# An encoder layer on one core: first loads in another order, the first mean of squares ahead of weight sums, the last scaling divided anew

## The chip, the cores and the metric

The kernel runs on one core of one Trainium2 chip. The metric is the device time of one execution in microseconds (us), lower is better. Before the change three runs took 1307.67, 1308.46 and 1308.58 us, median 1308.46.

## What is computed

One layer of a token mixer with two branches and a convolutional gated MLP, then a last RMSNorm, on 256 positions by 2048 columns in float32. Cut to what the change touches:

```python
def rms_norm(x, g):
    y = xf * lax.rsqrt(jnp.mean(xf * xf, axis=-1, keepdims=True) + RMS_EPS)
    return (y * g).astype(x.dtype)

h = rms_norm(x, g_norm)
proj = h @ w_in                     # 2048 x 9216: u, v | q, k, v | two gates
...                                 # gMLP branch, neighbourhood attention, merge
x = x + merged @ w_out
...                                 # norm, up-projection, width-3 convolution, SiLU gate
x = x + (silu(gate) * val) @ w_down
return rms_norm(x, norm_final)
```

## The kernel before

**Products.** Every factor in float32 is split into a high part (`whi` for weights, the first half of an `h` tile for activations) that TensorE multiplies at full rate, and the rest (`wlo`, the second half). A product is three matmuls: high x high, low x high, high x low. ACT makes the high part of a weight piece (line 151), then DVE subtracts it to get the low part (line 152).

**Weights come in pieces.** A list of pieces is planned ahead; `begin(i)` loads up to piece i + 5 (`LOAD_AHEAD`, five raw tiles `wraw`) and splits up to piece i + 4 (`SPLIT_AHEAD` is 3; four `whi` and four `wlo` tiles). For the first nine pieces the table `SPLIT_TO` says how far to split at each step. Loads all go out on SP's queue, in program order, except two that go on ACT's queue at the start. A function that is put on `preload[i]` is called just before the load of piece i, `at(i, f)` calls f when TensorE's program reaches piece i: before the splitting of that step for the first nine pieces, behind it later. Every engine works strictly in the order so written down, so an instruction that waits holds what stands behind it.

**The first stage** is `run_wide(g_v)`, the projection to v (pieces 0 to 15), then `run_wide(g_va)` (pieces 16 to 31). A piece is one block of 128 rows of `w_in` by 1024 columns; `V_ORDER` gives the order of the blocks: 0, 1, 6, 7, 8, 9 and so on. A plain piece is four triples, twelve matmuls. Two pairs of pieces in v (`V_QUADS`: pieces 10, 11 and 12, 13) and three in va are multiplied by a scheme with seven products instead of eight for a two by two arrangement of blocks. It needs sums of activation blocks (`act_sums`, lines 295 to 298, split by lines 314 and 315) and sums of weight blocks (`weight_sums`, lines 324 to 327; `weight_sums_split`, ACT line 334, DVE line 335). `X_SUMS` gives the steps of the activation sums; `wide` puts the weight sums of a pair three steps ahead of it and their split two steps ahead.

**The activations** come transposed: `x_t` has 128 partitions by 16 blocks of 256 positions, one block for each 128 rows of `w_in`. `x_split(k)` multiplies block k by its column of the norm vector `gmix` and splits it: high part on ACT (line 495), low part on DVE (line 496). `X_TURN` lists in what order and at which step pairs of blocks are split; the loads follow the same order. SP's first loads are x block 0, the two halves of piece 0, piece 1, x blocks 6 and 7, piece 2, x blocks 2 and 3, piece 3; ACT's queue has `gmix` and x block 1.

Until the first weights are there TensorE transposes an identity matrix `WAKE` times (`keep_awake`).

**The row scale** 1/sqrt(mean of squares) is applied to the results. `x_stats` squares x on ACT at steps 7 to 16; `x_norm` at step 17 (`NORM_AT`) sums the squares, scales them, lets ACT take the root and refines the inverse on DVE in `rstd` (lines 449 to 455). At step 17 `wide` also puts the weight sums of va's first pair, ahead of `x_norm`. The result is first used by the gelu of v at steps 18 and 21, on ACT.

**The end.** `finish(ps, t, c)` is called four times, as TensorE ends each of the last four accumulators (row half t, column half c of the last 1024 columns): it adds the residual (line 1023), squares on ACT with a sum (1026), multiplies by the norm vector (1063). When c is 1, the mean of squares of row half t is complete: the small chain in lines 1069 to 1074 gives `r` (inverse root) and `e` (a correction). `write` then multiplies all 2048 columns by `r` times `e` in five cuts, some on DVE, some on ACT, and stores five cuts, four on SP's queue and one on ACT's. Row half 0 is written while TensorE is still busy with row half 1.

Of the kernel before, what the change touches and what calls it, by code (L numbers as in the profile page):

```python
# [15 lines left out]
T = 256  # L16
D = 2048
# [46 lines left out]
def trunk_kernel(ctx, tc, x, x_t, vecs, w_in, ln_g, ln_b, w_st, b_s, rpb, w_branch, w_out, w_up, w_down,  # L64
# [105 lines left out]
    def at(i, f):  # L170
        tasks.setdefault(i, []).append(f)
# [92 lines left out]

    def wide(src, row0, order, c0, acts, quads, room, done, sums=None, odd=None, stored=None, split_room=None):
# [140 lines left out]

    xr = xin.tile([128, KD, T], F32, name="xr")

# [4 lines left out]
    def load_xt(k, n, queue=None):  # L413
        (queue or nc.sync).dma_start(xr[:, k:k + n], x_t[:, k:k + n])

    gmix = const.tile([128, KD], F32)
    gffn = const.tile([128, KD], F32)
    ck = const.tile([128, 4, 2 * NF], F32)
    nc.scalar.dma_start(gmix, vecs[:, 0:KD])
    load_xt(1, 1, nc.scalar)  # L420

    def load_late():
        nc.sync.dma_start(gffn, vecs[:, KD:2 * KD])
        nc.sync.dma_start(ck.rearrange("p a b -> p (a b)"), vecs[:, 2 * KD:])

# [17 lines left out]

    def rstd(name, ssum, n, eps):
        w = ssum.shape[-1]
        a = const.tile([128, w], F32, name=name + "_a")
        r = const.tile([128, w], F32, name=name + "_r")
        s = const.tile([128, w], F32, name=name + "_s")
        nc.vector.tensor_scalar(a, ssum, 1.0 / n, float(eps), op0=OP.mult, op1=OP.add)
        nc.scalar.activation(s, a, AF.Sqrt)  # L450
        nc.vector.reciprocal(r, s)
# [41 lines left out]
    def x_split(k):  # L493
        a, g = xT[k], gmix[:, k:k + 1]
        nc.scalar.activation(a[:, 0, :], xr[:, k], AF.Copy, scale=g)  # L495
        nc.vector.scalar_tensor_tensor(a[:, 1, :], xr[:, k], g, a[:, 0, :].bitcast(F32), op0=OP.mult, op1=OP.subtract)  # L496
# [559 lines left out]
    def finish(ps, t, c):  # L1056
        x2 = rs["x2"]
        add_down(ps[t][c], t, 2 + c)
        square_columns(t, 2 + c)
        if c == 0:  # L1060
            fin["y", t] = hpool.tile([128, 2, 512], F32, name=f"h{t}")
        y = fin["y", t]
        nc.vector.tensor_mul(y[:, c], x2[:, t, 1024 + c * 512:1536 + c * 512], fin["g", 2 + c])
        if c == 0:
            if t:
                fin["out"]()
            return
        a, r, q, e, pt, both = (const.tile([128, 1], F32, name=f"{n}3{t}") for n in "arqepb")
        nc.vector.tensor_scalar(pt, fin["ss"][:, t, 2:3], 1.0 / D, fin["part"][:, t:t + 1], op0=OP.mult, op1=OP.add)
        nc.vector.tensor_scalar(a, fin["ss"][:, t, 3:4], 1.0 / D, pt, op0=OP.mult, op1=OP.add)  # L1070
        nc.scalar.activation(q, a, AF.Sqrt)
        nc.vector.reciprocal(r, q)
        nc.vector.scalar_tensor_tensor(e, r, r, a, op0=OP.mult, op1=OP.mult)
        nc.vector.tensor_scalar(e, e, -0.5, 1.5, op0=OP.mult, op1=OP.add)

        def write():
            on_act = (3,) if t else (1, 3)
            cuts = (0, 256, 768, 1024, 1536, 2048)
            for n in (0, 1, 2, 3, 4):
                v = x2[:, t, cuts[n]:cuts[n + 1]]  # L1080
                u = y[:, n - 3] if n > 2 else v
                if n in on_act:
                    nc.scalar.activation(v, u, AF.Copy, scale=both)
                else:
                    nc.vector.tensor_scalar(v, u, r, e, op0=OP.mult, op1=OP.mult)
                if n == 0:
                    nc.vector.tensor_mul(both, r, e)
            for n in (0, 1, 2, 3, 4):
                (nc.scalar if n == 3 else nc.sync).dma_start(out[0, t * 128:(t + 1) * 128, cuts[n]:cuts[n + 1]],
                                                             x2[:, t, cuts[n]:cuts[n + 1]])  # L1090

        if t:
            write()
        else:
            fin["out"] = write
# [10 lines left out]
    def odd_room(name, dt):  # L1106
        return s_room["odd"].tile([128, 2, 512], dt, name=name)

    first_sums = {2 * q: {} for q, _, _ in X_SUMS}
# [71 lines left out]
    xsq = const.tile([128, NT, 4], F32)  # L1181
# [4 lines left out]
    def x_norm():  # L1186
        s = const.tile([128, NT], F32, name="ss1")
        nc.vector.tensor_reduce(s, xsq, axis=AX.X, op=OP.add)
        r = rstd("n1", s, D, RMS_EPS)
        st1["r"] = r  # L1190

# [150 lines left out]
```

## Time and profile before

| | |
|---|---|
| median of three runs | 1308.46 us |
| time of the profiled execution | 1307.83 us |
| its span, first to last instruction | 1306.0 us |
| TensorE busy | 1293.6 us, 99% of the span |
| VectorE (DVE) busy | 1072.5 us, 82% |
| ScalarE (ACT) busy | 776.8 us, 59% |
| granted TensorE clock, mean | 0.997 |
| moved by DMA | 277 MB, mean 212 GB/s |

In rows of the profile the engines are PE (TensorE's matmuls), PEld (its weight loads), DVE, ACT, POOL and SP; a q behind the name is the engine's sequencer, which issues DMAs. Rows of the timeline are: start in us, duration in us, engine, line, operation, output and inputs by the program's names, shape, count, and in brackets how long the engine had stood idle and what ended that. Rows of the waits are: who waited, for whom, us in total, times, longest. A row of windows is: stretch, its length, busy time and instructions of PE, PEld, DVE, ACT and POOL, the granted clock, the share of the DMA engines and GB/s. GB/s rows divide their window into 40 equal slices. Instructions of one engine overlap a little, so the distance from start to start is shorter than the duration.

### The profile page before, as it was taken

How to read it: one execution, taken by the hardware profiler on the slowest of the kernel's cores; microseconds unless marked ns; L12 is line 12 of the kernel's file. 1: busy time of each engine (PE TensorE's matmuls, PEld its weight loads, DVE VectorE, ACT ScalarE, POOL GpSimd, SP SyncE). 2: the span in 40 equal slices, each digit the busy share in tenths (PEclk: the TensorE clock that was granted, in tenths of full speed). 3: DMA queues.
4: the chain of work that ended last, by engine and by line, in shares of the span. 5: the costliest groups of instructions: out<-in, count | busy, mean ns of one | idle time of the engine just before them, and what ended most of it. 6: DMA issues, size and time to landing. Idle time of an engine off the chain costs nothing.

```text
span 1306.0 us, 19254 instructions
## 1 busy us (share of the span) xinstructions
PE 1293.6 (99%) x6712; PEld 1103.9 (85%) x6712; DVE 1072.5 (82%) x1616; ACT 776.8 (59%) x1153; POOL 104.7 (8%) x206
## 2 busy tenths in 40 slices
PE   9999999999999999999999999999999999999997
PEld 7888888888888888888888888888888888888885
DVE  7997777667689966986778878787888889999997
ACT  7766476666655644556556556565555656665563
POOL 0005405413000000000000000000000000000000
PEclk9999999999999999999999999999999999999998
DMA  9779657556556657565566566666666658876782
GB/s 351 251 243 258 191 166 214 175 171 195 177 170 204 218 182 248 202 211 163 177 195 209 182 211 198 215 194 212 191 211 199 215 161 286 288 267 227 265 290 105
DMA packets 174225, 277.19 MB, mean 212 GB/s; under 512 B 13488, under 2 KB 121904, under 8 KB 174128
## 3 DMA queue, kind: packets, MB, share of 16 engines
q1 hardware_dynamic: 165520, 252.28, 59.5%
q0 software_dynamic: 8032, 23.03, 5.5%
q8 instruction: 52, 0.85, 0.3%
q10 hardware_dynamic: 576, 0.66, 0.1%
q14 instruction: 45, 0.37, 0.1%
HBM read 266.48 MB, written 7.34 MB: 210 GB/s over the span
## 4 chain that ended last, share of the span: by engine, by line
PE 96%; DVE 1%; ACT 1%; DMA 1%; issue 0%; SPq 0%; ACTq 0%; DVEq 0%
PE bank L203 31%; PE bank L207 16%; PE bank L291 11%; PE bank L289 11%; PE bank L290 11%; PE bank L231 5%; PE bank L233 4%; PE bank L232 4%; DMA wraw<-in_w_in_dram 1%; PE bank L756 1%; PE bank L806 0%; DVE wlo L152 0%; PE bank L622 0%; PE bank L796 0%; PE bank L887 0%
## 5 line engine op out<-in xcount | busy, mean ns | idle before, releaser
L152 DVE TENSOR_TENSOR wlo<-wraw,whi 128x1024 fp32r<-128x1024 f32 (+1 forms) x472 | 546.0, 1170 | 182.5 <-ACT whi L151 100.4
L151 ACT ACTIVATE whi<-wraw 128x1024 fp32r<-128x1024 f32 (+1 forms) x472 | 470.3, 1010 | 218.4 <-PE bank L290 85.1
L203 PE MATMUL bank<-h,whi 128*128 128x512 f32 x1760 | 425.5, 392 | 0.0
L203 PEld LDWEIGHTS bank<-h,whi 128*128 128x128 f32 x1760 | 322.1, 188 | 61.7
L207 PEld LDWEIGHTS bank<-h,wlo 128*128 128x128 f32 x1760 | 225.9, 191 | 8.8
L207 PE MATMUL bank<-h,wlo 128*128 128x256 f32 x1760 | 228.6, 283 | 0.0
L985 ACT ACTIVATE tc<-ta,ck 128x256 f32<-128x256 f32 x86 | 47.1, 594 | 117.1 <-DVE ta L983 117.1
L291 PE MATMUL bank<-wlo,a 128*128 128x512 f32 x224 | 87.3, 390 | 0.0
L290 PE MATMUL bank<-whi,a 128*128 128x512 f32 x224 | 87.2, 389 | 0.0
L289 PE MATMUL bank<-whi,a 128*128 128x512 f32 x224 | 87.1, 389 | 0.0
L289 PE MATMUL bank<-whi,h 128*128 128x512 f32 x210 | 82.4, 393 | 0.6 <-ACT h L495 0.6
L291 PE MATMUL bank<-wlo,h 128*128 128x512 f32 x210 | 81.9, 390 | 0.7 <-DVE wlo L152 0.7
L290 PE MATMUL bank<-whi,h 128*128 128x512 f32 x210 | 81.8, 390 | 0.8 <-DVE h L496 0.8
L334 ACT ACTIVATE h<-h 128x1024 fp32r<-128x1024 f32 x40 | 40.2, 1053 | 33.7 <-DVE h L326 33.7
L988 DVE SCALAR_TENSOR_TENSOR tc<-ta,ck,tc 128x255 f32<-128x255 f32 x86 | 41.4, 481 | 14.4 <-ACT tc L985 14.4
L231 PE MATMUL bank<-whi,y 128*128 128x512 f32 x128 | 50.5, 394 | 0.0
L231 PE MATMUL bank<-whi,h 128*128 128x512 f32 x128 | 50.4, 394 | 0.0
L233 PE MATMUL bank<-wlo,h 128*128 128x512 f32 x128 | 49.9, 390 | 0.0
L233 PE MATMUL bank<-wlo,y 128*128 128x512 f32 x128 | 49.9, 390 | 0.0
L232 PE MATMUL bank<-whi,y 128*128 128x512 f32 x128 | 49.8, 389 | 0.0
L232 PE MATMUL bank<-whi,h 128*128 128x512 f32 x128 | 49.8, 389 | 0.0
L291 PEld LDWEIGHTS bank<-wlo,a 128*128 128x128 f32 x224 | 42.0, 188 | 9.1 <-DVE wlo L152 0.3
(284 smaller groups left out, 1786.0 us busy)
## 6 DMA issues: line engine op xcount, KB each, us to landing
wraw<-in_w_up_dram SPq DMA_DIRECT2D x336, 256.0 KB, 3.2
wraw<-in_w_in_dram SPq DMA_DIRECT2D x111, 512.0 KB, 4.5
wraw<-in_w_down_dram SPq DMA_DIRECT2D x86, 512.0 KB, 5.4
wraw<-in_w_in_dram SPq DMA_DIRECT2D x66, 256.0 KB, 3.3
wraw<-in_w_branch_dram SPq DMA_DIRECT2D x32, 512.0 KB, 4.6
wraw<-in_w_out_dram SPq DMA_DIRECT2D x32, 512.0 KB, 4.0
h<-sums POOLq DMA_DIRECT2D x20, 512.0 KB, 7.0
sums<-so POOLq DMA_DIRECT2D x10, 512.0 KB, 5.4
```

Of the source, the lines that this page charges most:

```text
L151: nc.scalar.activation(h[:, k, :m], w[:, k, :m], AF.Copy)
L152: nc.vector.tensor_sub(l[:, k, :m], w[:, k, :m], h[:, k, :m].bitcast(F32))
L203: nc.tensor.matmul(p, h[:, k - k0, b * 128:(b + 1) * 128], acts(k), start=k == 0, stop=k == nk - 1)
L207: nc.tensor.matmul(p[:, :T], l[:, k - k0, b * 128:(b + 1) * 128], acts(k)[:, 0, :], start=False, stop=False)
L231: nc.tensor.matmul(p, xh, h[:, kk, :m], start=st, stop=False)
L232: nc.tensor.matmul(p, xl, h[:, kk, :m], start=False, stop=False)
L233: nc.tensor.matmul(p, xh, l[:, kk, :m], start=False, stop=sp)
L289: nc.tensor.matmul(p, xh, h, start=st, stop=False)
L290: nc.tensor.matmul(p, xl, h, start=False, stop=False)
L291: nc.tensor.matmul(p, xh, l, start=False, stop=sp)
L985: nc.scalar.activation(v, u, AF.Identity, scale=ck[:, 1, ch:ch + 1], bias=ck[:, 3, ch:ch + 1])
L988: nc.vector.scalar_tensor_tensor(v[:, 1:], u[:, :T - 1], ck[:, 0, ch:ch + 1], v[:, 1:], op0=OP.mult, op1=OP.add)
```

## The change

Three places.

1. **First loads.** The norm vector `norm_mix` is put in front of the rows of `x_t` by the host (16 columns, so a row has 4112 instead of 4096 elements). Block 0 is loaded with it on ACT's queue in one DMA, ahead of block 1; the separate load of `gmix` goes, and SP begins with the weights of piece 0. Blocks 6 and 7 are loaded and split one by one, around piece 2; blocks 2, 3 and 4, 5 come behind blocks 8 to 11. The high part of block 0 is made on DVE. The activation sums of v's first pair move from steps 3 and 4 to steps 5 and 6, those of the second from 6 and 9 to 7 and 10. The weight sums of v's second pair, and their split, come a step later (`late`). There are 14 wake transposes instead of 17.
2. **Mean of squares.** `rstd` is cut in two. `root` (scale and root) is registered ahead of the weight sums of step 17, `inverse` behind them.
3. **Last scaling.** The root takes the mean's factor and the rest of the sum as scale and bias, so that it no longer follows a DVE instruction; the first part of the sum is made a call earlier; the product of `r` and `e` stands ahead of the scaling. DVE scales 768 and 512 columns, ACT 512 and 256, and there are three stores (768 and 512 columns on SP, 768 on ACT) for each row half instead of five.

```diff
-WAKE = 17
+WAKE = 14
-X_TURN = ((0, 0), (3, 1), (1, 2), (4, 2), (5, 3), (2, 4), (6, 6), (7, 9))
-SPLIT_TO = (3, 4, 4, 7, 8, 8, 11, 12, 12)
+X_TURN = ((0, 0), (3, 1), (4, 2), (5, 3), (1, 4), (2, 5), (6, 6), (7, 9))
+SPLIT_TO = (2, 4, 4, 7, 8, 8, 11, 12, 12)
-X_SUMS = ((1, 3, 4), (2, 6, 9), (6, 18, 19))
+X_SUMS = ((1, 5, 6), (2, 7, 10), (6, 18, 19))
...
-            at(i - 3, lambda i=i, b=b: weight_sums(i, b, room))
-            at(i - 2, lambda b=b, own=own: weight_sums_split(b, own))
+            j = i - 2 if q in late else i - 3
+            at(j, lambda i=i, b=b: weight_sums(i, b, room))
+            at(j + 1, lambda b=b, own=own: weight_sums_split(b, own))
...
-    xr = xin.tile([128, KD, T], F32, name="xr")
+    xall = xin.tile([128, KD + KD * T], F32, name="xr")
+    gmix, xr = xall[:, :KD], xall[:, KD:].rearrange("p (k t) -> p k t", t=T)
...
-        (queue or nc.sync).dma_start(xr[:, k:k + n], x_t[:, k:k + n])
-
-    gmix = const.tile([128, KD], F32)
+        c = slice(KD + k * T if k else 0, KD + (k + n) * T)
+        (queue or nc.sync).dma_start(xall[:, c], x_t[:, c])
+
-    nc.scalar.dma_start(gmix, vecs[:, 0:KD])
+    load_xt(0, 1, nc.scalar)
     load_xt(1, 1, nc.scalar)
...
-    def rstd(name, ssum, n, eps):
-        w = ssum.shape[-1]
-        a = const.tile([128, w], F32, name=name + "_a")
-        r = const.tile([128, w], F32, name=name + "_r")
-        s = const.tile([128, w], F32, name=name + "_s")
+    def root(name, ssum, n, eps):
+        a, r, s = (const.tile([128, ssum.shape[-1]], F32, name=f"{name}_{c}") for c in "ars")
         nc.vector.tensor_scalar(a, ssum, 1.0 / n, float(eps), op0=OP.mult, op1=OP.add)
         nc.scalar.activation(s, a, AF.Sqrt)
+        return a, r, s
+
+    def rstd(name, ssum, n, eps):
+        return inverse(*root(name, ssum, n, eps))
+
+    def inverse(a, r, s):
         nc.vector.reciprocal(r, s)
...
-        nc.scalar.activation(a[:, 0, :], xr[:, k], AF.Copy, scale=g)
+        if k:
+            nc.scalar.activation(a[:, 0, :], xr[:, k], AF.Copy, scale=g)
+        else:
+            nc.vector.tensor_scalar(a[:, 0, :], xr[:, k], g, None, op0=OP.mult)
...
             if t:
                 fin["out"]()
+            pt = fin["pt", t] = const.tile([128, 1], F32, name=f"p3{t}")
+            nc.vector.tensor_scalar(pt, fin["ss"][:, t, 2:3], 1.0 / D, fin["part"][:, t:t + 1], op0=OP.mult, op1=OP.add)
             return
-        a, r, q, e, pt, both = (const.tile([128, 1], F32, name=f"{n}3{t}") for n in "arqepb")
-        nc.vector.tensor_scalar(pt, fin["ss"][:, t, 2:3], 1.0 / D, fin["part"][:, t:t + 1], op0=OP.mult, op1=OP.add)
-        nc.vector.tensor_scalar(a, fin["ss"][:, t, 3:4], 1.0 / D, pt, op0=OP.mult, op1=OP.add)
-        nc.scalar.activation(q, a, AF.Sqrt)
+        pt, ss = fin["pt", t], fin["ss"][:, t, 3:4]
+        a, r, q, e, both = (const.tile([128, 1], F32, name=f"{n}3{t}") for n in "arqeb")
+        nc.scalar.activation(q, ss, AF.Sqrt, scale=1.0 / D, bias=pt)
+        nc.vector.tensor_scalar(a, ss, 1.0 / D, pt, op0=OP.mult, op1=OP.add)
         nc.vector.reciprocal(r, q)
         nc.vector.scalar_tensor_tensor(e, r, r, a, op0=OP.mult, op1=OP.mult)
         nc.vector.tensor_scalar(e, e, -0.5, 1.5, op0=OP.mult, op1=OP.add)
+        nc.vector.tensor_mul(both, r, e)
 
         def write():
-            on_act = (3,) if t else (1, 3)
-            cuts = (0, 256, 768, 1024, 1536, 2048)
-            for n in (0, 1, 2, 3, 4):
...
-            for n in (0, 1, 2, 3, 4):
-                (nc.scalar if n == 3 else nc.sync).dma_start(out[0, t * 128:(t + 1) * 128, cuts[n]:cuts[n + 1]],
-                                                             x2[:, t, cuts[n]:cuts[n + 1]])
+            v = x2[:, t]
+            o = out[0, t * 128:(t + 1) * 128]
+            for u, w in ((v[:, :768], v[:, :768]), (y[:, 1], v[:, 1536:])):
+                nc.vector.tensor_scalar(w, u, r, e, op0=OP.mult, op1=OP.mult)
+            for u, w in ((y[:, 0], v[:, 1024:1536]), (v[:, 768:1024], v[:, 768:1024])):
+                nc.scalar.activation(w, u, AF.Copy, scale=both)
+            nc.sync.dma_start(o[:, :768], v[:, :768])
+            nc.sync.dma_start(o[:, 1536:], v[:, 1536:])
+            nc.scalar.dma_start(o[:, 768:1536], v[:, 768:1536])
...
+    def x_root():
+        s = const.tile([128, NT], F32, name="ss1")
+        nc.vector.tensor_reduce(s, xsq, axis=AX.X, op=OP.add)
+        st1["root"] = root("n1", s, D, RMS_EPS)
+
+    def x_norm():
+        st1["r"] = inverse(*st1["root"])
+
+    at(NORM_AT, x_root)
     first_sums = {2 * q: {} for q, _, _ in X_SUMS}
     g_v = wide(w_in2, 0, V_ORDER, V0, xt, V_QUADS, first_room, (ev_v_sums, ev_v), first_sums,
-               odd_room)
+               odd_room, late=V_QUADS[1:])
...
-    preload[0] = [lambda: load_xt(0, 1)]
-    for n, (c, _) in enumerate(X_TURN[1:]):
-        preload[n + 2] = [lambda c=c: load_xt(2 * c, 2)]
+    first_chunk = X_TURN[1][0]
+    preload[2] = [lambda: load_xt(2 * first_chunk, 1)]
+    preload[3] = [lambda: load_xt(2 * first_chunk + 1, 1)]
+    for n, (c, _) in enumerate(X_TURN[2:]):
+        preload.setdefault(n + 4, []).append(lambda c=c: load_xt(2 * c, 2))
...
-    for c, i in X_TURN[1:]:
+    at(1, lambda: x_split(2 * first_chunk))
+    at(1, lambda: split_to(3))
+    at(1, lambda: x_split(2 * first_chunk + 1))
+    for c, i in X_TURN[2:]:
         at(i, lambda c=c: x_chunk(c))
```

More of the change, by code (lines that the diff above doesn't have):

```diff
@@ L260, in run_group, with wide @@
             done(ps, b)
-    def wide(src, row0, order, c0, acts, quads, room, done, sums=None, odd=None, stored=None, split_room=None):
+    def wide(src, row0, order, c0, acts, quads, room, done, sums=None, odd=None, stored=None, split_room=None, late=()):
         n0 = plan_wide(src, row0, order, c0)
@@ L413, in load_xt @@
     def load_xt(k, n, queue=None):
-        (queue or nc.sync).dma_start(xr[:, k:k + n], x_t[:, k:k + n])
-    gmix = const.tile([128, KD], F32)
+        c = slice(KD + k * T if k else 0, KD + (k + n) * T)
+        (queue or nc.sync).dma_start(xall[:, c], x_t[:, c])
     gffn = const.tile([128, KD], F32)
     ck = const.tile([128, 4, 2 * NF], F32)
-    nc.scalar.dma_start(gmix, vecs[:, 0:KD])
+    load_xt(0, 1, nc.scalar)
     load_xt(1, 1, nc.scalar)
     def load_late():
-        nc.sync.dma_start(gffn, vecs[:, KD:2 * KD])
-        nc.sync.dma_start(ck.rearrange("p a b -> p (a b)"), vecs[:, 2 * KD:])
+        nc.sync.dma_start(gffn, vecs[:, :KD])
+        nc.sync.dma_start(ck.rearrange("p a b -> p (a b)"), vecs[:, KD:])
     def load_ws():
@@ L1074, in finish @@
         nc.vector.tensor_scalar(e, e, -0.5, 1.5, op0=OP.mult, op1=OP.add)
+        nc.vector.tensor_mul(both, r, e)
         def write():
-            on_act = (3,) if t else (1, 3)
-            cuts = (0, 256, 768, 1024, 1536, 2048)
-            for n in (0, 1, 2, 3, 4):
[L1080 to L1087, printed above, removed]
-            for n in (0, 1, 2, 3, 4):
-                (nc.scalar if n == 3 else nc.sync).dma_start(out[0, t * 128:(t + 1) * 128, cuts[n]:cuts[n + 1]],
-                                                             x2[:, t, cuts[n]:cuts[n + 1]])
+            v = x2[:, t]
[7 more added lines that the diff above has]
+            nc.scalar.dma_start(o[:, 768:1536], v[:, 768:1536])
         if t:
@@ L1107, in odd_room @@
         return s_room["odd"].tile([128, 2, 512], dt, name=name)
+    xsq = const.tile([128, NT, 4], F32)
+    def x_root():
[5 more added lines that the diff above has]
+    at(NORM_AT, x_root)
     first_sums = {2 * q: {} for q, _, _ in X_SUMS}
     g_v = wide(w_in2, 0, V_ORDER, V0, xt, V_QUADS, first_room, (ev_v_sums, ev_v), first_sums,
-               odd_room)
+               odd_room, late=V_QUADS[1:])
     g_va = wide(w_in2, 0, VA_ORDER, VA0, xt, VA_QUADS, first_room, (ev_va_sums, ev_va), first_sums)
@@ L1326 @@
     laid = dict(inputs)
-    laid["x_t"] = _np.asarray(inputs["x"])[0].T.reshape(KD, 128, T).transpose(1, 0, 2)
-    laid["vecs"] = _np.concatenate([columns(n) for n in ("norm_mix", "norm_ffn", "conv_k", "conv_b")], axis=1)
+    x_t = _np.asarray(inputs["x"])[0].T.reshape(KD, 128, T).transpose(1, 0, 2).reshape(128, KD * T)
+    laid["x_t"] = _np.concatenate([columns("norm_mix"), x_t], axis=1)
+    laid["vecs"] = _np.concatenate([columns(n) for n in ("norm_ffn", "conv_k", "conv_b")], axis=1)
     laid["w_st"] = _np.asarray(inputs["gm_w_s"])[0].transpose(2, 0, 1)
```

6 lines of the change are left out of this document (removed).

## The prediction

> **What bounds the kernel now.** I read the page first (busy shares, chain of waits), then who waited for whom on TensorE, then both ends in order of time, since the change touches only the first 70 us and the last 13.
>
> ```profile
> PE 1293.6 (99%) x6712; PEld 1103.9 (85%) x6712; DVE 1072.5 (82%) x1616; ACT 776.8 (59%) x1153; POOL 104.7 (8%) x206
> PE 96%; DVE 1%; ACT 1%; DMA 1%; issue 0%; SPq 0%; ACTq 0%; DVEq 0%
> PE bank L290 <- DVE h L496: 0.8, 1, 0.8
> PE bank L291 <- DVE wlo L152: 0.7, 2, 0.5
> PE bank L289 <- ACT h L495: 0.6, 1, 0.6
> 1297.00:1306.00 9.00, 0.01 (x1) 0.00 (x0) 3.98 (x12) 2.16 (x5) 0.00 (x0) 0.64 0.65 232
> ```
>
> TensorE (PE) sets the end: 99% busy, 96% of the chain. No matmul is removed, so the change can win only the time before the first product, four small waits and the last 9 us, in which PE does nothing. Here are the start and the four waits (a piece is 128 rows of w_in by 1024 columns, twelve products; whi and wlo are its two halves by precision, h those of an x block).
>
> ```profile
> 1.37 3.89 PE L440 MATMUL bank<-ident 128*128 128x128 f32 x17 [1.37 <-POOL ident masks.py:199]
> 4.54 0.63 ACT L151 ACTIVATE whi<-wraw 128x512 fp32r<-128x512 f32 x1 [0.84 <-DMA wraw<-in_w_in_dram]
> 5.23 0.78 PE L289 MATMUL bank<-whi,h 128*128 128x512 f32 x1
> 10.34 1.06 ACT L151 ACTIVATE whi<-wraw 128x1024 fp32r<-128x1024 f32 x1 [2.44 <-DMA wraw<-in_w_in_dram]
> 11.85 0.50 PE L289 MATMUL bank<-whi,h 128*128 128x512 f32 x1 [0.59 <-ACT h L495]
> 13.11 0.50 PE L290 MATMUL bank<-whi,h 128*128 128x512 f32 x1 [0.75 <-DVE h L496]
> 19.21 0.50 PE L291 MATMUL bank<-wlo,h 128*128 128x512 f32 x1 [0.16 <-DVE wlo L152]
> 42.01 0.39 PE L289 MATMUL bank<-h,y 128*128 128x512 f32 x1
> 42.46 0.39 PE L291 MATMUL bank<-l,y 128*128 128x512 f32 x1
> 67.13 0.50 PE L291 MATMUL bank<-wlo,h 128*128 128x512 f32 x1 [0.53 <-DVE wlo L152]
> ```
>
> Products start 0.227 us apart (42.01 and 42.46 are two steps) and last 0.39, so a wait costs its idle time plus 0.16 (0.27 at 13.11, after a 0.50 one), plus 0.1 for the restart (0.50 instead of 0.39). The three early waits thus cost 0.75 + 1.02 + 0.32 and three restarts, 2.4 us; the one at 67 costs 0.69 + 0.1. The start waits for the first weights (4.54), PE following 0.69 later.
>
> **The first loads.** Before, SP issues x block 0 ahead of the weights; afterwards block 0, with the norm vector in its rows, goes out on ACT's queue in the vector's place, and SP begins with the weights.
>
> ```profile
> 0.75 0.38 SPq L414 DMA_DIRECT2D xr<-in_x_t_dram  x1
> 1.19 0.89 SPq L124 DMA_DIRECT2D wraw<-in_w_in_dram  x2
> GB/s 0 36 206 284 409 377 213 270 377 430 406 424 401 426 412 420 406 426 397 414 424 430 418 375 391 412 408 299 315 344 258 381 414 401 352 363 346 84 182 344
> ```
>
> The weights move up one issue slot, 1.19 - 0.75 = 0.44. ACT still has two issues ahead of its table load, so that does not move. The first hi of x goes to DVE, idle then; it is off ACT's path. First product: 5.23 - 0.44 = 4.79. Fourteen wake transposes end at 1.37 + 14 x 0.229 = 4.58, so they do not hold it. Bounds: 0 if the two queues share the start of the stream badly, 0.6 if ACT's freed 0.5 shows; I take 0.44.
>
> Piece 2 now follows one x block, not two: 131 KB less at about 420 KB/us (the last row, one slice per us) is 0.31, so it lands at 10.34 - 0.44 - 0.31 = 9.6. ACT's hi ends at 10.65, DVE's wlo runs 10.67 to 11.89. Both halves of block 6 are already there. PE, which reaches piece 2 at 11.10 - 0.44 = 10.66, starts at once and waits 0.8 at the third product, against 1.77 before. Piece 3 (landed about 1.07 earlier) and piece 4 are in time, so 19.21's wait goes too. PE's lead by 20 us is 0.44 + 1.0 + 0.42, about 1.8 us.
>
> **Where that lead goes.** From 11.43 to 65 us DVE hardly rests: in this stage it is the second bound.
>
> ```profile
> 20.00:30.00 10.00, 10.00 (x46) 8.26 (x45) 9.90 (x18) 6.71 (x13) 0.00 (x0) 1.00 0.99 382
> 11.43 1.22 DVE L152 TENSOR_TENSOR wlo<-wraw,whi 128x1024 fp32r<-128x1024 f32 x1 [2.73 <-ACT whi L151]
> 14.50 1.67 DVE L496 SCALAR_TENSOR_TENSOR h<-xr,gmix,h 128x256 fp32r<-128x256 f32 x4
> 16.09 0.28 DVE L295 TENSOR_TENSOR y<-y 128x128 f32<-128x128 f32 x1
> 17.14 0.88 DVE L496 SCALAR_TENSOR_TENSOR h<-xr,gmix,h 128x256 fp32r<-128x256 f32 x2
> 25.72 2.95 DVE L152 TENSOR_TENSOR wlo<-wraw,whi 128x1024 fp32r<-128x1024 f32 x3
> 37.66 0.68 DVE L315 TENSOR_TENSOR y<-y,y 128x512 fp32r<-128x512 f32 x1
> 38.26 0.87 DVE L496 SCALAR_TENSOR_TENSOR h<-xr,gmix,h 128x256 fp32r<-128x256 f32 x2
> 40.19 2.35 DVE L335 TENSOR_TENSOR l<-y,h 128x1024 fp32r<-128x1024 f32 x2
> ```
>
> From start to start: an x lo 0.40 (14.50 to 16.09, four), the four small sums of an x pair 1.05 (16.09 to 17.14), L315 0.60 (37.66 to 38.26), a full wlo 1.14 (a pair lasts 2.35, one 1.22). In the changed order DVE does, between the wlo of pieces 2 and 8, six wlo (6.8), eleven x lo (4.4), one set of small sums (1.05) and one L315 (0.6): 12.85 us. It must also wait. ACT now splits x 10 and 11 ahead of piece 4, and these land after x 7, piece 3, x 8-9 and piece 4, 1.70 MB or 4.05 us behind piece 2, at 13.65; two hi (0.8) and piece 4's hi (1.06) later it is 15.5, while DVE was done at 15.0. With that 0.5 and some 0.5 of single steps behind ACT (pieces 6 and 8, blocks 12 and 13), the wlo of piece 8 starts at 10.67 + 12.85 + 1.0 = 24.5: 1.2 ahead of 25.72.
>
> But behind it DVE meets work that had stood ahead: the second x pair's small sums (1.05), and the wlo of piece 14, which now stands before the weight-sum splits (L335) of pieces 12 and 13 (1.14). PE needs the first of those splits for the product at 42.46. Before, it was ready at 40.19 + 1.22 = 41.41, 15.7 after 25.72; now at 24.5 + 15.7 + 1.05 + 1.14 = 42.4. So PE, about 1.8 early, stands until 42.4 and goes on as before: its lead there is about 0. What hid the late sums was the 1.05 of slack, and it is used up. The late sums also hold the raw tiles of pieces 12 and 13 about 1.7 us longer; the loads behind them on SP (pieces 17, 18) still land near 42, before DVE can use them (45).
>
> **The mean of squares.** Before, DVE issues n_a after the weight sums and stands until ACT's root is back; everything behind it is late by that.
>
> ```profile
> 57.62 0.17 DVE L449 TENSOR_SCALAR n_a<-ss 128x2 f32<-128x2 f32 x1
> 58.06 0.17 DVE L451 RECIPROCAL n_r<-n_s 128x2 f32<-128x2 f32 x1 [0.27 <-ACT n_s L450]
> 61.41 0.91 ACT L305 ACTIVATE y<-xr,gmix 128x256 f32<-128x256 f32 x2 [0.53 <-DVE y L335]
> 65.86 1.22 DVE L152 TENSOR_TENSOR wlo<-wraw,whi 128x1024 fp32r<-128x1024 f32 x1 [2.29 <-ACT whi L151]
> ```
>
> Afterwards the root runs on ACT under the four weight sums (2.5 us), so its 0.27 is hidden; without that cover it would be paid again. DVE reaches this point 0.1 ahead (1.2 - 1.05, rounded down; piece 14's wlo is moved, not added). L305 waits for DVE, the gelu stands behind it on ACT, piece 22's hi behind that, and PE at 67.13 for its wlo: all come 0.1 + 0.27 = 0.37 earlier. DVE and PE move alike after that, and no later wait exists. **Front: -0.37.** Its bounds are in the rivals.
>
> **The last scaling.** After the last product (DVE starts on it at 1297.05):
>
> ```profile
> 1297.54 0.35 ACTq L1089 DMA_DIRECT2D out_dram<-x  x1
> 1297.94 0.63 ACT L1026 ACTIVATE junk<-x 128x512 f32<-128x512 f32 x1 [0.43 <-DVE x L1023]
> 1298.70 0.21 DVE L1070 TENSOR_SCALAR a<-ss,p 128x1 f32<-128x1 f32 x1
> 1298.95 0.20 ACT L1071 ACTIVATE q<-a 128x1 f32<-128x1 f32 x1 [0.28 <-DVE a L1070]
> 1299.83 0.41 DVE L1085 TENSOR_SCALAR x<-x,r,e 128x256 f32<-128x256 f32 x1
> 1300.27 0.33 SPq L1089 DMA_DIRECT2D out_dram<-x  x1
> 1301.71 0.40 SPq L1089 DMA_DIRECT2D out_dram<-x  x1
> GB/s 377 295 33 0 0 0 0 0 57 303 328 303 58 328 328 344 410 426 377 344 410 377 377 344 345 328 360 410 377 377 393 360 295 33 0 0 0 0 0 0
> ```
>
> The root takes mean and bias by itself: `a` leaves the path (1298.70 to 1298.95, -0.25), and an x2 square no longer starts behind ACT's store issue at 1297.54, which now comes before it is ready (-0.15, 1297.94 to 1297.79). A column scalar as operand adds about 0.09 to the root: by L151's two sizes (1.06, 0.63) a 256-column copy without one takes 0.42, and L305, which has one, about 0.5 (0.91 for two that overlap). `both` now stands ahead of the scaling, +0.08, and the first store waits for 768 columns, about 0.68, instead of 256, 0.41. The first store thus leaves at 1300.27 - 0.25 - 0.15 + 0.09 + 0.08 + 0.27, about 1300.3: no earlier. The last leaves near 1300.85 instead of 1301.71, but the last row (slices of 0.125 us from 1300) shows the queue full from 1301.0 to 1304.2: 1.05 MB, 327 KB/us, with a hole at 1301.5 and slower parts. Three large stores without holes at 380 take 2.76 instead of 3.2. **Tail: -0.4**; bounds 0 (no better drain) and -0.9 (the last issue's full gain), nearer the drain because the queue is what is full.
>
> **Sum.** -0.37 - 0.4, about -0.8: the profiled execution, 1307.83 us with its span of 1306.0 inside, becomes 1307.0. That one lies 0.63 under the median shown (1308.46), so the forecast is 1307.6.
>
> [...]
>
> **Rivals.** *Faster: the slow patch in the stream vanishes.* Slices 6 and 7 moved 213 and 270 KB where neighbours move 420: 0.85 us lost ahead of piece 2. If reading x with its new pitch cures it, DVE and the splits come 0.85 earlier: front -1.2, tail -0.4 to -0.9: 1306.5. For it: x blocks 6 and 7 are in flight there, and their pitch changes from 16384 to 16448 bytes. Against: later x blocks have the same pitch and the slices from 9 on show no such hole. [...]
>
> *Slower: DVE falls behind.* If the stream comes no earlier than before, piece 8's wlo starts at 25.72, the sums' first split is ready at 43.6, PE stands 1.2 us there, and DVE is 1.05 - 0.27 = 0.8 late at 67: with no gain in the tail 1309.2. It decides when that wlo starts after 24.9 (25.72 - 0.78). For it: my estimate is only 0.4 from that point. Against: the issue slot (0.44) and the bytes (0.31), which no engine can take back.
>
> *It does not do what it says:* the early waits stay because ACT still gates piece 2; then 1308.1, the tail alone.
>
> **How the numbers follow.** Forecast (with the third rival beside it) 0.55, the faster rival 0.28, the slower 0.12, more than these 0.05. Less than 0.2% (2.6 us), about what the measurement cannot tell from no change, is 1305.84 to 1311.08. All of the faster rival's best ends (front also without DVE's 1.0 of waiting, tail -0.9) give 1305.4. Faster by more: 0.18; slower by more: 0.06; within: 0.76. Range 1305.4 to 1309.2.
>
> **What would show it.** Right: first product near 4.8; waits at piece 2 under 1 us; a new wait of 1 to 1.8 us on the split of the weight sums near 42; the wait near 67 shorter; no 0.27 before the reciprocal; last store issued before 1301 by the old clock, landing little earlier. Wrong: no wait near 42, or DVE with pauses over 2 us between 12 and 25, or a first product after 5.2.

## The result and the profile after

| kernel | median, us | range | runs |
|---|---|---|---|
| before | 1308.26 | 1307.20 to 1309.16 | 22 |
| after | 1310.33 | 1309.54 to 1311.87 | 22 |

After divided by before is 1.0017, interval 1.0011 to 1.0023: the change costs about 2 us. My forecast was 1307.6 with a range up to 1309.2. The profiled execution of after took 1311.06 us with a span of 1309.25, so profile against profile the difference is 3.2 us.

First the page of after, and who waited for whom on TensorE (total, times, longest).

```profile
PE 1296.0 (99%) x6709; PEld 1102.9 (84%) x6709; DVE 1073.4 (82%) x1614; ACT 777.4 (59%) x1153; POOL 104.6 (8%) x206
...
PE bank L291 <- DVE y L316: 1.2, 1, 1.2
PE bank L292 <- DVE l L336: 1.1, 1, 1.1
PE bank L203 <- DVE ya L634: 0.8, 1, 0.8
PE bank L290 <- ACT whi L151: 0.4, 1, 0.4
```

The number to stop at is the first: TensorE is busy 1296.0 us, where before it was 1293.6, with the same products and three wake transposes fewer. Idle time is not in that number, so some matmuls may have become slower. A comparison stage by stage must tell which, since slow first products (0.78 us at 5.23 before) and the restart after a wait (0.50 us at 40.97 in after, where the next last 0.40) count as busy too (e1 below is busy 1294.9 us with its branch products as fast as before). The three old waits at 11.85, 13.11 and 19.21 are gone, two new ones (L316, L336) stand near 41 and 43, and a third, at line 203, stands at 141.

The timeline of after at the steps that the prediction named (start, duration, engine, line; in brackets the idle time and what ended it):

```profile
5.03 0.50 PE L290 MATMUL bank<-whi,h 128*128 128x512 f32 x1 [0.41 <-ACT whi L151]
8.97 1.06 ACT L151 ACTIVATE whi<-wraw 128x1024 fp32r<-128x1024 f32 x1 [0.50 <-DMA wraw<-in_w_in_dram]
24.65 1.23 DVE L152 TENSOR_TENSOR wlo<-wraw,whi 128x1024 fp32r<-128x1024 f32 x1 [0.26 <-ACT whi L151]
26.09 1.83 DVE L152 TENSOR_TENSOR wlo<-wraw,whi 128x1024 fp32r<-128x1024 f32 x2 [0.22 <-ACT whi L151]
28.89 0.70 DVE L326 TENSOR_TENSOR y<-y,wraw 128x512 f32<-128x512 f32 x1 [0.37 <-DMA wraw<-in_w_in_dram]
40.97 0.50 PE L291 MATMUL bank<-whi,y 128*128 128x512 f32 x1 [1.19 <-DVE y L316]
41.97 2.36 DVE L336 TENSOR_TENSOR l<-y,h 128x1024 fp32r<-128x1024 f32 x2
43.24 0.50 PE L292 MATMUL bank<-l,y 128*128 128x512 f32 x1 [1.07 <-DVE l L336]
58.36 0.16 DVE L456 RECIPROCAL n_r<-n_s 128x2 f32<-128x2 f32 x1
66.07 1.23 DVE L152 TENSOR_TENSOR wlo<-wraw,whi 128x1024 fp32r<-128x1024 f32 x1 [2.29 <-ACT whi L151]
67.35 0.50 PE L292 MATMUL bank<-wlo,h 128*128 128x512 f32 x1
141.51 0.74 PE L203 MATMUL bank<-h,whi 128*128 128x512 f32 x2 [0.81 <-DVE ya L634]
```

The product of 67.13 now starts at 67.35: the front, meant to win 0.37, loses 0.22. The wait at 141 costs 0.81 plus 0.26 by the prediction's own price. The reciprocal at 58.36 has no idle time before it any more.

Then the slower matmuls. Windows of the two kernels over the same stretch of the branch products (lines 231 to 233: a y block is the stationary operand, the weights' halves are streamed past it), before and then after; columns: stretch, length, PE busy and its matmuls, PEld, DVE, ACT, POOL, granted clock, DMA share, GB/s.

```profile
465.00:510.00 45.00, 45.00 (x204) 37.36 (x203) 28.76 (x34) 20.04 (x22) 1.20 (x2) 1.00 0.60 194
```

```profile
465.00:510.00 45.00, 45.00 (x199) 36.34 (x198) 27.95 (x32) 19.77 (x22) 0.00 (x0) 1.00 0.58 186
```

TensorE is busy all the time in both, its clock is 1.00 in both, and it does 199 matmuls instead of 204: 2.5% slower, 5 x 0.227 = 1.1 us in this stretch alone. By their starts these products are 0.233 us apart instead of 0.227, about 350 of them in the trace. Products of the same three lines with an h block as the stationary operand keep their 0.227.

The tail, timeline and the DMA rate in 40 slices of 0.131 us from 1304:

```profile
1301.00 0.69 DVE L1031 TENSOR_TENSOR x<-bank,x 128x512 f32<-128x512 f32 x1
1304.22 0.33 SPq L1094 DMA_DIRECT2D out_dram<-x  x1
1304.79 0.35 ACTq L1096 DMA_DIRECT2D out_dram<-x  x1
GB/s 0 0 0 0 0 0 0 23 374 421 328 351 468 445 374 320 328 406 437 374 398 414 351 445 398 375 375 374 211 0 0 0 0 0 0 0 0 0 0 0
```

The last accumulator is ready at 1301.00 instead of 1297.05: 3.95 late. The end is 3.2 late, so the tail wins 0.75. In sum: front +0.22, wait at 141 +1.07, slower branch products +2.3 (the same product is 1.6 late at 340 us and 3.9 late at 510), 0.4 in small steps, tail -0.75: 3.2.

### The profile page after: what moved, and what is told of

Same layout as the page of the kernel before. It is cut to its first block, busy times and chain, and to the rows that moved or that the text cites. A ratio compares the mean times of both kernels' runs of the same rounds, so it can differ in the third digit from the quotient of the medians.

```text
span 1309.3 us, 19236 instructions
## 1 busy us (share of the span) xinstructions
PE 1296.0 (99%) x6709; PEld 1102.9 (84%) x6709; DVE 1073.4 (82%) x1614; ACT 777.4 (59%) x1153; POOL 104.6 (8%) x206
## 4 chain that ended last, share of the span: by engine, by line
PE 93%; DMA 3%; DVE 2%; ACT 1%; issue 1%; ACTq 0%; DVEq 0%
PE bank L203 29%; PE bank L207 15%; PE bank L292 11%; PE bank L290 11%; PE bank L291 11%; PE bank L231 5%; PE bank L233 5%; PE bank L232 5%; DMA wraw<-in_w_in_dram 2%; DVE wlo L152 1%; ACT whi L151 1%; PE bank L764 1%; PE bank L814 0%; DMA xr<-in_x_t_dram 0%; PE bank L967 0%
```

## The experiments

One thing in the diff is not about time at all: the tile `gmix` leaves the pool `const`, which is laid out ahead of weights, activations and all else on its side of the memory. Sixteen floats are 64 bytes. As the program lays them out, the high halves of the weights start at 26880 (105 x 256) before and at 26816 after; the y blocks hang at the other end and stay at 192256 (751 x 256), put there by the unused tile `Y_GAP`. **Theory A** says that this shift slows the branch products. **Rival B** says the new order of the work does it, **rival C** that it is scatter between executions.

Medians of all runs, each with the kernel before in the same series:

| run | median, us | before | ratio, interval |
|---|---|---|---|
| e1_pad | 1307.33 | 1308.21 | 0.9996, 0.9987 to 1.0005 |
| e2_before_shift | 1311.13 | 1308.21 | 1.0023, 1.0013 to 1.0034 |
| e3_y_too | 1308.72 | 1308.21 | 1.0005, 0.9996 to 1.0014 |
| e4_tail_alone | 1307.39 | 1308.21 | 0.9996, 0.9987 to 1.0005 |
| e5_split_now | 1308.79 | 1308.11 | 1.0003, 0.9994 to 1.0012 |
| e6_root_alone | 1308.05 | 1308.11 | 1.0000, 0.9991 to 1.0009 |
| e7_y_down_128 | 1310.62 | 1308.11 | 1.0019, 1.0010 to 1.0028 |
| e8_y_up_64 | 1310.68 | 1308.11 | 1.0020, 1.0010 to 1.0029 |
| e9_pad_again | 1307.73 | 1308.41 | 0.9996, 0.9987 to 1.0005 |
| e10_old_loads | 1306.75 | 1308.41 | 0.9989, 0.9980 to 0.9998 |
| e11_old_pitch | 1309.39 | 1308.41 | 1.0009, 0.9999 to 1.0018 |
| e12_small_sums_pool | 1309.15 | 1308.41 | 1.0005, 0.9996 to 1.0014 |
| e13_old_sums | 1307.54 | 1308.29 | 0.9993, 0.9984 to 1.0002 |
| e14_old_loads_again | 1307.19 | 1308.29 | 0.9990, 0.9981 to 0.9999 |
| e15_packed_old_order | 1306.70 | 1308.29 | 0.9987, 0.9978 to 0.9995 |

An interval reaches about 1.2 us to each side. What moves 2.5 us or more stands by the times alone; for the rest the profile has to carry the reading.

**e1: the 64 bytes put back**

```diff
     gffn = const.tile([128, KD], F32)
+    const.tile([128, KD], F32, name="pad")
```

> The kernel after, with an unused 64-byte tile put into the const pool in the place that the norm vector had there, so that every buffer behind it (raw, high and low weights, h, y windows of v) has the address it had before the change; the loads, the order and the tail stay as changed. Theory A (the 64-byte shift slows the products with stationary y and the DMAs of the v windows): the products of the branch stages start 0.227 us apart again and the wait of 1.08 at 141 us shrinks or goes, so the time falls by 2.4 to 3.5 us, to 1306.9 to 1308.0. Rival B (the changed order of the loads and sums does it, addresses do nothing): 1310.3 again, within 0.5. Rival C (the difference of those stages between the two profiles is scatter between executions): 1310.3 by the timed rounds too.

1307.33: 3.0 less than after, by an unused tile. The same windows row for e1:

```profile
465.00:510.00 45.00, 45.00 (x204) 37.36 (x203) 28.79 (x34) 20.19 (x23) 0.00 (x0) 1.00 0.63 192
```

204 matmuls again. The wait at 141 stayed (1.2), which theory A had wrong.

**e2: the shift alone, in the kernel before**

```diff
-    gmix = const.tile([128, KD], F32)
+    gmix = xin.tile([128, KD], F32, name="gmix")
```

> The kernel before, with one edit: the tile of the norm vector is taken from the pool of x instead of const, so that every buffer behind const lies 64 bytes lower, as after the change. No instruction and no load moves. Theory A: branch products 0.231 to 0.236 us apart (+2.4) and a wait near 141 us (+0 to 1.1): 1310.7 to 1311.8 where before is 1308.3. Rivals B and C: 1308.3 within 0.5.

1311.13, +2.9, with no instruction moved in the program. Its row:

```profile
465.00:510.00 45.00, 45.00 (x199) 36.36 (x198) 28.22 (x32) 19.45 (x23) 0.00 (x0) 1.00 0.59 187
```

B and C fall: nothing but addresses differs, and the loss is there.

**e3, e7, e8: which address?** Only the unused tile at the y blocks changes: e3 is after with `Y_GAP = 288` (y moved down with the weights), e7 and e8 are before with 352 (y down 128) and 160 (y up 64).

> The kernel after, with the unused tile behind the y blocks 64 bytes larger (288 for 224), so that the y blocks are moved down by the same 64 bytes as the weights; nothing else differs. If the distance between the two operands of the branch products counts (A1): steps of 0.227 there, 2.4 us less than after, 1307.4 to 1308.5. If the weights' or y's own place counts (A2: the high parts of the weights start at 192 modulo 256): no gain or a further loss, 1310.3 or more. The wait at 141 us stays in both if it comes from the place of the raw weights or of the v windows.

> The kernel before with the y blocks 128 bytes lower (unused tile behind them 352 for 224), nothing else. If every distance between y and the weights that is not a multiple of 256 bytes slows the branch products: steps of 0.231 to 0.236 there and 1310.5 to 1311. If the pattern repeats after 128 bytes: steps of 0.227 and 1308.2.

> The kernel before with the y blocks 64 bytes higher (unused tile 160 for 224), nothing else: the weights stay where they were and the y blocks leave the multiple of 256, with the same distance between the two as in the kernel after. If the distance counts: steps of 0.231 to 0.236 in the branch stages and 1310.5 to 1311. If the weights' own place at 192 modulo 256 was what slowed them: steps of 0.227 and 1308.2.

The rows of e3, e7 and e8, in this order:

```profile
465.00:510.00 45.00, 45.00 (x204) 37.34 (x203) 28.80 (x34) 20.05 (x22) 0.00 (x0) 1.00 0.61 192
```

```profile
465.00:510.00 45.00, 45.00 (x199) 36.52 (x198) 27.75 (x33) 20.01 (x22) 0.00 (x0) 1.00 0.59 186
```

```profile
465.00:510.00 45.00, 45.00 (x199) 36.36 (x197) 27.63 (x32) 19.81 (x22) 0.00 (x0) 1.00 0.60 186
```

With both at 192 modulo 256 the products are fast (e3), with a distance of 64 or 128 they are slow, whichever of the two operands stands on the multiple of 256 (2.5 us slower in e7 and e8). So the distance between the streamed and the stationary operand counts, not the place of one. Tried were distances of 0, of 128 and of 64 with the weights the lower of the two modulo 256 (weights moved down in after and e2, y moved up in e8); 64 the other way was not. Why the distance counts no run shows, nor with what period: 256 is only the number by which I count the addresses. e3 is 1.6 us under after where 1.8 to 2.9 were expected; its one profile met a fall of the clock (last section), but one execution can't say how much of the median that is.

**The wait at 141** was part of my theory A, and that part is wrong. It shows in the profiles of e4 and e6, whose weights lie where they lay before, and it is there in one of two executions of the same program: none in e10's profile, and in e14's:

```profile
PE bank L203 <- DVE ya L629: 1.0, 1, 1.0
```

In 17 profiles it is missing six times, and up to 2.1 us long. Profile against profile, 1 us of the 3.2 was therefore scatter; that fits the medians, which differ by 2.1.

**e4 and e6: last scaling alone, mean of squares alone**, each put into the kernel before as in the diff above.

> The kernel before with the last scaling of the change alone (root with scale and bias, three cuts, three stores). The two profiles give the tail -0.74 us, my forecast gave -0.4 (0 to -0.9): 1307.5, between 1307.3 and 1307.9, where before is 1308.3. If the -0.74 hangs on where the front leaves the engines: 1308.3.

> The kernel before with the mean of squares alone changed (root ahead of the weight sums of step 17, the inverse behind them); nothing is moved in memory. Forecast of my prediction: the vector engine's 0.27 us idle is hidden and the wait near 67 is 0.27 shorter: 1307.9 where before is 1308.2. If the root on the scalar engine now holds something behind it there: 1308.2 or more.

e4 took 0.82 less than before, though its interval includes zero. The profiles settle the tail: from the start of the last product to the end of the span it is 9.40 to 9.42 us in the five profiles with the old tail and 8.68 to 8.73 in the twelve with the new one. e6 took as long as before; its profile meets the wait at 141 with 2.1 us, and half the clock behind it (last section).

The wlo that stood at 65.86 before (about 2.3 us idle ahead of it in the rows shown here) is a mark of the front. For a small edit it is too coarse: e4, whose front is before's, has it at 65.20, and e6 no earlier:

```profile
65.22 1.22 DVE L152 TENSOR_TENSOR wlo<-wraw,whi 128x1024 fp32r<-128x1024 f32 x1 [2.29 <-ACT whi L151]
```

The wait of TensorE right behind it does show the edit, here in e4 and in e6:

```profile
66.48 0.50 PE L291 MATMUL bank<-wlo,h 128*128 128x512 f32 x1 [0.53 <-DVE wlo L152]
```

```profile
66.50 0.50 PE L291 MATMUL bank<-wlo,h 128*128 128x512 f32 x1 [0.29 <-DVE wlo L152]
```

It is 0.52 to 0.53 us in the five profiles with the old loads and the old root, and 0.26 to 0.29 in the three with the old loads and the new root (e6, e10, e14): about 0.25 is won there. The times of e6 are too coarse for that.

**e5 and e12: relieving the wait near 42** (both with the 64 bytes put back). In e5 the split of the late sums follows the sums in the same step; in e12 the small sums of three x pairs go to GpSimd.

```diff
-            at(j + 1, lambda b=b, own=own: weight_sums_split(b, own))
+            if q not in late:
+                at(j + 1, lambda b=b, own=own: weight_sums_split(b, own))
...
+    for q in V_QUADS[1:]:
+        at(2 * q - 2, lambda b=g_v[5][q]: weight_sums_split(b, odd_room))
```

```diff
-        nc.vector.tensor_sub(s3, a11, a21)
+        eng.tensor_sub(s3, a11, a21)
...
+                   eng=nc.gpsimd if early else nc.vector)
```

> The kernel after with the 64 bytes put back (as the first run of this study, 1307.33), and the split of the weight sums of v's second pair put right behind the split of the x sums in step 10, ahead of the low part of piece 14, instead of a step later. The first low part of the sums is then ready about 1.1 us earlier (42.0 instead of 43.15). Theory D (in the front the vector engine is the second bound up to the gelu; a stall of the products removed near 42 comes back at 67): the wait near 42 falls from 0.8 to nearly nothing, another of about 1 us appears near 67, and the time stays: 1307.3 within 0.5. Rival E (the wait near 42 is the front's only loss and nothing behind it takes its place): 1306.2.

> The kernel after with the 64 bytes put back, and the four small sums of each of the three early x pairs (1.05 us a pair) on GpSimd instead of the vector engine. Theory D (the vector engine binds the front up to 67 us): it is about 1 us earlier at the weight sums and 2 to 3 us less busy by 67; the waits near 42 and 67 shrink and the time falls by about 1, to 1306.3. If the front isn't bound there, or GpSimd's sums come too late: 1307.3 or more.

e5, TensorE at the end of the front:

```profile
66.15 0.50 PE L291 MATMUL bank<-whi,h 128*128 128x512 f32 x1 [1.18 <-ACT whi L151]
...
67.41 0.50 PE L293 MATMUL bank<-wlo,h 128*128 128x512 f32 x1 [0.52 <-DVE wlo L152]
```

TensorE was 1.9 us earlier than e1 at 43 and had lost it all by 67, as theory D said: 67.41 against after's 67.35. The time that went with it, 1307.3, was missed: why e5's median is 1.1 to 1.5 us over e9's and e1's the profiles don't show.

e12 took 1309.15 where 1306.3 was hoped for. Its GpSimd and DVE rows:

```profile
20.22 1.12 POOL L296 TENSOR_TENSOR y<-y 128x128 f32<-128x128 f32 x1 [18.91 <-ACT y L306]
...
22.63 0.46 POOL L299 TENSOR_TENSOR y<-y 128x128 f32<-128x128 f32 x1
23.79 0.69 DVE L317 TENSOR_TENSOR y<-y,y 128x512 fp32r<-128x512 f32 x1 [1.56 <-ACT y L316]
```

Four small sums take GpSimd 2.9 us (20.22 to 23.09) and DVE 1.05, and DVE stands 1.56 for them.

**e11: the old pitch.** After, with x rows unpadded and the norm vector loaded by itself on GpSimd's queue.

```diff
+    gmix = const.tile([128, KD], F32)
...
+    nc.gpsimd.dma_start(gmix, vecs[:, 0:KD])
```

> The kernel after, but the norm vector is loaded by itself on the idle GpSimd queue into its old tile in const, and the rows of x have their old pitch of 16384 bytes; the order of the other loads is the new one, and the buffers have their old addresses. If the new pitch cured the slow patch of the stream at 6 to 8 us: the patch is back (a slice of 1 us near 210 KB), piece 2 lands 0.8 later than 8.95. If the order of the loads cured it: piece 2 lands near 9.0. The time in both cases about that of the run with the pad, 1307.3 to 1308, because the vector engine takes the lead back by 67 us.

```profile
6.93 0.77 PE L290 MATMUL bank<-whi,h 128*128 128x512 f32 x1 [2.31 <-ACT h L501]
...
8.84 1.06 ACT L151 ACTIVATE whi<-wraw 128x1024 fp32r<-128x1024 f32 x1
```

Piece 2 is there by 8.84 with the old pitch, as with the new one (8.97): in this order the pitch cures nothing. The vector came late on that queue, the first product started 1.9 us after after's, and the time rose by 1.66 over e9: what was lost at the very start was not won back (at 67 us e11 is 2.4 behind e9).

**e9, e10, e13 to e15: the order of the first loads.** All have the old addresses, the new mean of squares and the new tail. e9 repeats e1 (new loads, late sums); e13 is e1 with the sums at their old steps; e10 and e14 have loads and sums as before; e15 has them as before too, but with the norm vector packed into x's rows and block 0 loaded and split as in the change. First e13 against e1, then e15 against e10:

```diff
-X_SUMS = ((1, 5, 6), (2, 7, 10), (6, 18, 19))
+X_SUMS = ((1, 5, 6), (2, 6, 9), (6, 18, 19))
-               odd_room, late=V_QUADS[1:])
+               odd_room)
```

```diff
-    gmix = const.tile([128, KD], F32)
+    const.tile([128, KD], F32, name="pad")
...
-    nc.scalar.dma_start(gmix, vecs[:, 0:KD])
+    load_xt(0, 1, nc.scalar)
     load_xt(1, 1, nc.scalar)
...
-    preload[0] = [lambda: load_xt(0, 1)]
```

> The kernel of the first run once more (after with the 64 bytes put back), beside the next three. Its first time was 1307.33, against 1308.79 for the kernel whose split of the sums was moved, in another session. If the first value holds: 1307.3 within 0.4, about 0.9 under before. If it was a lucky session: 1308.3 to 1308.8. Its profile has, or has not, the wait of 1.1 near 141 us; if that wait is scatter between executions and not the layout, it can be missing this time.

> The kernel before with the new mean of squares and the new last scaling; loads, splits and sums of the first stage stay as before, and memory too. The difference to the run beside it (pad again) is what the new order of the first loads is worth. My prediction gave it -0.1 (1.2 earlier on the vector engine, 1.05 of it used up): then this is 0.1 slower than the run beside it, 1307.4. If the late sums cost more than the earlier loads bring: 0.5 to 1 us faster than the run beside it.

> The kernel after with the 64 bytes put back, and the sums of v's second pair at their old steps (x sums at 6 and 9, weight sums at 9, their split at 10, ahead of the low part of piece 14); the loads stay in the new order. If the late sums are what the front loses by (their split at 43.0 instead of 41.4): the wait near 42 goes, nothing takes its place, 1306.7 where the kernel with the late sums is 1307.3 to 1307.7. If the front is held by several bounds one behind the other (stream, buffers of high parts, vector engine): the wait is found again at 67 or before, 1307.3 to 1308.

> The kernel before with the new mean of squares and the new last scaling, once more (1306.75 before, 1.66 under the kernel before it and 0.98 under the one with the new loads). If that holds: 1306.5 to 1307.0. By the sum of the parts measured one by one (-0.82 and -0.06): 1307.3.

> As the run beside it (new mean of squares, new last scaling), with the norm vector packed in front of x, block 0 and its high part as in the change and 14 wake transposes, 64 bytes put back; all other loads, splits and sums in the old order. If the first product comes 0.25 earlier and that lasts: 0.25 faster than the run beside it. If block 1, which then lands later (5.5 for 4.9), takes it back: the same, or up to 0.5 slower. The slow patch of the stream tells whether the new pitch alone moves it: with it, piece 2 lands near 9.9 instead of 10.2; without, near 9.0.

New loads 1307.73 and 1307.54, old loads 1306.75 and 1307.19, old order with the packed vector 1306.70. The mark of the front in e9, e13 and e15:

```profile
65.86 1.23 DVE L152 TENSOR_TENSOR wlo<-wraw,whi 128x1024 fp32r<-128x1024 f32 x1 [2.29 <-ACT whi L151]
```

```profile
65.74 1.23 DVE L152 TENSOR_TENSOR wlo<-wraw,whi 128x1024 fp32r<-128x1024 f32 x1 [2.29 <-PE bank L292]
```

```profile
64.73 1.23 DVE L152 TENSOR_TENSOR wlo<-wraw,whi 128x1024 fp32r<-128x1024 f32 x1 [2.29 <-ACT whi L151]
```

Before has 65.86, with the old root; e10 and e14, with the old loads and the new root, have 65.33 and 65.13. So the new loads win nothing: beside these two they stand 0.4 to 0.7 us later, with late sums or without. In e13 the wait on the late sums near 42 is gone, and TensorE waits for low parts of weights instead, near 41 and 67:

```profile
PE bank L292 <- DVE wlo L152: 1.9, 2, 1.4
```

The packed vector in the old order stands 0.4 to 0.6 ahead of e10 and e14. The mark scatters by as much, so that gain is not shown, and the medians do not part the three.

Whom DVE waits for between 11.5 and 64.5 us (an instruction that runs into this window counts with the wait ahead of it); before, e9 and e15:

```profile
DVE wlo L152 <- ACT whi L151: 2.7, 1, 2.7
DVE n_r L451 <- ACT n_s L450: 0.3, 1, 0.3
```

```profile
DVE wlo L152 <- ACT whi L151: 1.8, 4, 0.7
```

```profile
DVE wlo L152 <- ACT whi L151: 1.6, 1, 1.6
```

In the old order DVE waits once, for piece 2, and then runs through (before has the root's 0.3 as well). In the new order it starts on piece 2 earlier still, at 9.85 in e9 behind 0.8 us of waiting that this row leaves out. But it stands four times later on (near 12, 15, 24 and 27 us) for a high part that ACT has not made yet. From piece 2's wlo to the mark it takes 54.0 and 54.1 us in e10 and e15, and 56.0 and 55.9 in e9 and e13: the 1.5 us that the new order is ahead of e10 at piece 2 are spent there, and more. e15 has the lowest median, 0.9987 of before and 3.6 us under after, but it can't be told from e10 and e14, which leave the first loads as they were.

## Why the prediction was wrong

**The failed step** is in its first paragraph: "No matmul is removed, so the change can win only the time before the first product, four small waits and the last 9 us." I costed what each instruction and load does and took the products' 0.227 us as given. What I left out is that the diff also moves tiles: it puts 64 bytes between streamed weights and stationary y, modulo 256. That costs +2.9 us by e2 and +2.6 by e8 (128 bytes: +2.5 by e7). Without it the whole change is e1 and e9, 1307.33 and 1307.73, where I forecast 1307.6. That agreement is partly luck. The front was to win 0.37 at the product of 67.13, and there e1 is 0.2 late and e9 level with before; the tail was to win 0.4 and won 0.73. The two misses nearly cancel.

**Start.** Forecast 4.79, measured 5.03. That is 0.20 won in this pair of profiles, but the first product scatters: it starts at 5.23 to 5.67 in the eight profiles with the old loads, of which before's is the earliest, and at 4.68 to 5.08 in the seven with the new ones (without e11). Median against median 0.6 is won, the upper bound I had named.

**Piece 2 and the early waits.** Landed at 8.97, not 9.6, and the three waits went: right, and more. The rival in which the pitch of x cures the slow patch is refuted by e11; e15, with the new pitch in the old order, has piece 2 at 9.56, just ahead of the 9.68 to 10.34 of the eight profiles with the old loads. What the new pitch of 16448 bytes costs or wins by itself no run isolates; e15, which has it, is as fast as any (1306.70).

**DVE.** Piece 8's wlo forecast 24.5, measured 24.65: right, and ahead of the 24.9 from which the slower rival was to decide. The first split of the late sums forecast 42.4, measured 41.97 + 1.22 = 43.2. I had carried the 15.7 us between the two over from before, where DVE never paused; now it pauses 0.22 for ACT and 0.37 for the landing of piece 11 (28.89). So TensorE stood 1.19 and 1.07, its whole lead and 1 us more.

**Mean of squares.** The 0.27 is hidden, as said, and with the old loads it shows at 67 (0.53 to 0.29). In after it was eaten by the item above: +0.22 instead of -0.37.

**Tail.** First store at 1300.3 and last at 1300.85 on the old clock, measured 1304.22 - 3.95 = 1300.27 and 1300.84: right. The drain takes 21 slices, 2.7 us (forecast 2.76), so the forecast's 0.4 is there. Missing in the sum was what follows it: the last bytes leave at 1307.75, 1.5 us ahead of the end of the span, where before it was about 1.9 (1304.2 to 1306.05). I had taken that rest as fixed; with it the tail is -0.75 in this pair, and -0.73 over all profiles. Why it is shorter with three stores than with five was not tried.

## What to carry to other kernels

Read a diff for what it does to the allocation too: a small tile added to or removed from a pool moves everything behind it, and here that cost more than every edit won (2.9 us by e2). When TensorE's busy time rises with the same matmuls at a full clock, compare the matmuls per window stage by stage, and look at the distance of the two operands; pad one side until it fits (3.0 us in e1). And an earlier first load was worth here what the next engine did with it without a pause (the 1.5 us won at piece 2 were spent by 67): follow that engine's idle time up to the next stage, not to the first product.

## What the runs showed of the hardware

**Operand distance.** With the addresses of the stationary and the streamed operand 64 or 128 bytes apart when counted modulo 256, a 512-column product took 2.5% longer (199 for 204 in 45 us; after, e2, e7 and e8 beside before, e1 and e3) at a granted clock of 1.00. The runs show this effect, and not its mechanism.

**The clock after short waits.** In e3's profile TensorE stood twice for 1.1 us, as in after, and then got half its clock. Windows of e3 (the column behind POOL is the granted clock):

```profile
41.00:43.00 2.00, 0.93 (x5) 0.45 (x3) 2.00 (x3) 2.00 (x5) 0.00 (x0) 1.00 0.90 348
43.00:44.00 1.00, 1.00 (x3) 0.78 (x4) 1.00 (x2) 1.00 (x2) 0.00 (x0) 0.68 1.07 410
44.00:45.00 1.00, 1.00 (x4) 0.78 (x3) 1.00 (x1) 1.00 (x3) 0.00 (x0) 0.50 0.96 370
...
46.00:47.00 1.00, 1.00 (x4) 0.76 (x4) 1.00 (x2) 0.59 (x3) 0.00 (x0) 0.62 0.74 96
```

The nine products from 43.26 to 46.91 start up to 0.43 us apart instead of 0.23, 1.6 us in all, on top of the waits; 1.0 of it was still there at 67. e6's profile shows the same behind its single wait of 2.05 us at 141, from 143.3 to 146.7:

```profile
144.00:145.00 1.00, 1.00 (x4) 0.71 (x4) 1.00 (x2) 0.41 (x2) 1.00 (x3) 0.50 0.87 284
```

Other executions kept 1.00: after with waits of 1.19 and 1.07, e12 with 1.27 and 1.08, e2 with a single one of 1.6. So e3's waits cost 1.6 us on top of their 2.2, and after's, as long, met no fall of the clock; what decides it these runs don't show. The clock fell behind 2.2 us of idle time in two parts in e3, and behind 2.05 in one in e6.

**The rate at the start.** The change also has 14 wake transposes for 17. In e1, e9 and e15 TensorE starts only 7 or 8 products between 7 and 10 us, most of them 0.43 us apart, where after has 12 and before 14. At 20 us e1 leads before by 0.2 us and after leads it by 2.0, and at 43 both are 0.9 behind it, so the front was not held by that. All eight profiles with 17 transposes have 12 to 14, but so have five with 14; whether fewer transposes bring the slow start was not tried.
